# One product per block for both gates of the RG-LRU, smaller side steps and a later modulation deadline in a two-layer hybrid backbone

## The chip, the cores and the metric

The kernel runs on one core of a Trainium2 chip. The metric is the device time of one launch in microseconds: 1726.16 us is the median of three runs (1722.91 to 1727.71). TensorE (PE) multiplies matrices, with its weight loads shown apart (PEld); VectorE (DVE), ScalarE (ACT) and GpSimd (POOL) work on tiles in SBUF, DVE and ACT also on the banks of PSUM that PE writes; SyncE (SP) issues most of the loads.

## What is computed

Two layers with shared structure run over 384 tokens: 128 context tokens and 256 latent tokens. Each layer projects the normalized, modulated tokens (1024 wide) to 10240 columns, runs four branches (A neighbourhood attention, B differential attention, C retention, D RG-LRU), weighs each branch's projection by a sigmoid gate, sums them, multiplies by `w_out`, adds the residual, and then runs a squared-ReLU MLP. The part that the change rewrites is branch D:

```
def rglru_gates(x, wa, ba, wx, bx, lam):
    xb = xf.reshape(b, t, LRU_BLOCKS, -1)          # 8 blocks of 64 channels
    r = sigmoid(einsum('btnd,nde->btne', xb, wa).reshape(b, t, w) + ba)
    i = sigmoid(einsum('btnd,nde->btne', xb, wx).reshape(b, t, w) + bx)
    log_a = -LRU_C * r * softplus(-lam)
    a = exp(log_a)
    u = sqrt(-expm1(2.0 * log_a)) * (i * xf)
    return a, u
# h[t] = a[t] * h[t-1] + u[t], once forward and once backward; hd = h_f + h_b
```

`xf` is the input after a centred convolution of four taps. The modulation (shift, scale and gain from `silu(cond) @ ada_w + ada_b`) is a matrix-vector product for each of the two token groups.

## The kernel before, in words

**Products.** All big products (projections, gates, branches, `w_out`, MLP) are done in three passes on split operands: a float32 weight `raw` is cut into a high part `wh` and a rest `wl`, the tokens are held as `hh` and `hl` (or `yh`, `yl` for branch outputs), and PE adds hh·wh, hl·wh and hh·wl. ACT or DVE makes `wh`, DVE makes `wl`. Weights come in loads of 1 MB into two `raw` buffers, on SP's queue; a load is issued when the buffer before last has been split.

**Banks.** PSUM has six banks with the tag `y` and two with the tag `mm`. The projections and the branch products go to `mm`: PE can work on one bank while DVE or ACT reads the other, and it starts a third group only when the first has been read. In the gate and branch products ACT makes `th` (the tanh of a gate) out of its bank, and DVE makes `acc` or `th` times the branch product out of another.

**The stream and the side steps.** A list of pieces in a fixed order (`run_stream`) issues the big products. Everything else, attention, retention, RG-LRU and modulation, is written as Python generators (`later`, `active`); `poll` advances them between the pieces, up to their next `yield`. It decides by a model of the engines' clocks (`Clock`, `Engine.cost`): it takes no step while DVE or ACT stand more than `BACKLOG` = 2.25 us ahead of PE in that model. What a generator issues between two yields is one step, and stands in each engine's queue without anything between. Each engine runs its queue in order, so the order is fixed when the program is built. `drain_side(tag)` finishes all steps with a tag: a deadline.

**RG-LRU.** `lx_evac` copies a projection out of its bank and convolves it on DVE (one multiply, three multiply-adds) into `setB_x`. For each of four pairs of blocks j and two directions d, `lru_tile` makes two gates m; each gate has one bank, and two products of 64x64 weights, which lie at the two diagonal corners of the array (`tile_position=(r, r)`). ACT applies tanh with the bias `hb` to 128 partitions, then come exp, tanh, square and square root on ACT and the two recurrences on DVE (`tensor_tensor_scan`). Multiply, scans, sums and the product with the gelu gate are one step. The gate weights lie in the tiles `bia`.

**Modulation.** `ada` streams `ada_w` in pieces of 256 KB into `half` tiles and accumulates on DVE (`big<-half,condT,big`); `ada_end` sums over the partitions on PE (`ones`), adds the bias, transposes. `need_y` of the layer's last branch drains it and issues the loads of the residual tokens (`load_x_tile`, three of 512 KB) and of the gains (`gain_tiles`, four of 256 KB); both are used after the product with `w_out`, whose last four slices are done by `out_tail`.

Of the kernel before, what the change touches and what calls it, by code (L numbers as in the profile page):

```python
# [140 lines left out]
class Engine:  # L141


    def __init__(self, clock, raw, key):
        self.clock, self.raw, self.key = clock, raw, key

    def __getattr__(self, name):
        f = getattr(self.raw, name)
# [18 lines left out]
    def cost(self, name, aps, k):  # L167
        if name == "dma_start":
            return 0.06
        n = max(_size(x) for x in aps)  # L170
        psum = any(x.space == PSUM for x in aps)
        if self.key == "ACT":
            return (0.05 if psum else 0.094) + n / 1200 + 0.09 * (len(aps) - 2)
        if self.key == "POOL":
            if k.get("op") == ALU.pow:
                return 0.3 + 0.16 * n
            return 0.1 + n / (290 if name == "tensor_copy" else 470)
        if self.key == "PE":
            n = _size(aps[0])
            if name == "transpose":  # L180
                return 0.107
            if aps[1].dtype == F32R:
                return max(n / 2195, 0.107)
            return max(n / 585, 0.22) * (aps[0].shape[0] / 128 if "tile_position" in k else 1)
        if name == "reciprocal":
            return 0.07 + n / 120
        extra = 0.06 * sum(x.shape[-1] == 1 for x in aps[1:])
        if name in ("tensor_scalar", "tensor_copy") and not psum:
            return 0.07 + n / 1920 + extra
        return 0.07 + n / 960 + extra  # L190
# [8 lines left out]
def hybrid_flow_kernel(ctx: ExitStack, tc: tile.TileContext, I, O):  # L199
# [162 lines left out]
    def stage_params():  # L362
# [72 lines left out]
        for l in range(DEPTH):  # L435
            pp = pps[l]
            li = 0.8 - 0.6 * math.exp(-0.3 * l)
            nlam = cp.tile([128, 1], F32, name=f"nlam{l}")
            dve.tensor_sub(nlam, e2[:, 2 * l + 1:2 * l + 2], e2[:, 2 * l:2 * l + 1])
            dve.tensor_scalar(nlam, nlam, -li, None, op0=ALU.add)  # L440
            hb = cp.tile([128, 24], F32, name=f"hb{l}")
            dve.tensor_scalar(hb, pp[:, R_BAF:R_BAF + 24], 0.5, None, op0=ALU.mult)
            dn = cp.tile([128, 1], F32, name=f"dn{l}")
            dve.tensor_scalar(dn, pp[:, R_DN:R_DN + 1], 1.0 - li, None, op0=ALU.mult)
            rn = cp.tile([128, 4], F32, name=f"rn{l}")
            dve.tensor_scalar(rn, pp[:, R_RN:R_RN + 4], 0.5, None, op0=ALU.mult)
# [10 lines left out]
            LP[l].update(nlam=nlam, hb=hb, dn=dn, rn=rn, lg=lg, nlb=nlb, lgc=lgc, zt=zt,  # L457
                         kl=lp[:, 32 + 8 * l:40 + 8 * l].rearrange("p (d j) -> p d j", d=2))
            yield

# [473 lines left out]
    def add_layer(l):  # L934
# [206 lines left out]
        def lx_evac(j, p):  # L1141
            xp = atile()
            pool.memset(xp[:, 0:1], 0.0)
            pool.memset(xp[:, 129:131], 0.0)
            pool.memset(xp[:, 387:389], 0.0)
            dve.tensor_copy(xp[:, 1:129], p[:, 0:128])
            dve.tensor_copy(xp[:, 131:387], p[:, 128:384])
            xd = ctile("setB_x")
            cw = lambda i: P("pp")[:, R_CW + 4 * i + j:R_CW + 4 * i + j + 1]
            dve.tensor_scalar(xd[:, 0:NL], xp[:, 0:NL], cw(0), P("pp")[:, R_CB + j:R_CB + j + 1], op0=ALU.mult, op1=ALU.add)  # L1150
            for i in range(1, 4):
                dve.scalar_tensor_tensor(xd[:, 0:NL], xp[:, i:NL + i], cw(i), xd[:, 0:NL], op0=ALU.mult, op1=ALU.add)
            S["xd"][j] = xd

        def gelu(a, gv):
# [17 lines left out]
            if j == 3:  # L1173
                later(S["split_yD"](), "yD")

        def lru_w(m):

            return S["bia"][m][:, 128:384].rearrange("p (j e) -> p j e", j=4)

        def lru_load():  # L1180
            S["bia"] = [stile([128, 640], "bia", 4) for _ in range(4)]
            for b in S["bia"]:
                pool.memset(b[:, 0:128], 0.0)
                pool.memset(b[:, 512:640], 0.0)
            for m, n in enumerate(("lru_wa_fwd", "lru_wx_fwd", "lru_wa_bwd", "lru_wx_bwd")):
                SP.dma_start(lru_w(m), I[n][l].rearrange("(j q) d e -> (q d) j e", q=2))

        def lru_tile(j):
            xd = S["xd"][j][:, 0:NL]
            while "kl" not in LP[l]:  # L1190
                yield
            yield (xd, *S["bia"])
            hst = S["hst"]
            A, U, Sq = [], [], []
            for d in range(2):
                base = 12 * d
                ths = []
                for m in range(2):
                    p = bank()[:, 0:NL]
                    w = lru_w(2 * d + m)  # L1200
                    for r in (slice(0, 64), slice(64, 128)):
                        mm(p[r], w[r, j], xd[r], start=True, stop=True, tile_position=(r.start, r.start))
                    th = tmp()[:, 0:NL]
                    act(th, p, AF.Tanh, scale=0.5, bias=P("hb")[:, base + 4 * m + j:base + 4 * m + j + 1])
                    ths.append(th)
                kl = P("kl")[:, d, j:j + 1]
                L, u = ths
                yield (L, u)
                dve.tensor_scalar(L, L, kl, kl, op0=ALU.mult, op1=ALU.add)
# [16 lines left out]
            for d in range(2):  # L1226
                u = U[d]
                dve.tensor_mul(u, u, Sq[d])
                h = Sq[d]
                st = P("pp")[:, (R_SF, R_SB)[d] + j:(R_SF, R_SB)[d] + j + 1]  # L1230
                for s, init in ((slice(0, 128), 0.0), (slice(130, 386), st)):
                    aa, uu, oo = A[d][:, s], u[:, s], h[:, s]
                    if d:
                        aa, uu, oo = aa[:, ::-1], uu[:, ::-1], oo[:, ::-1]
                    dve.tensor_tensor_scan(oo, aa, uu, init, ALU.mult, ALU.add)
                hs.append(h)
            pool.tensor_copy(hst[:, j:j + 1], hs[0][:, 127:128])
            pool.tensor_copy(hst[:, 4 + j:5 + j], hs[1][:, 0:1])
            gg = S["gg"][j]
            for s, o in ((slice(0, 128), slice(0, 128)), (slice(130, 386), slice(128, 384))):  # L1240
                dve.tensor_add(hs[0][:, s], hs[0][:, s], hs[1][:, s])
                dve.scalar_tensor_tensor(gg[:, o], hs[0][:, s], 0.5, gg[:, o], op0=ALU.mult, op1=ALU.mult)
            S["yD"][j] = gg[:, 0:NTOK]
            if j == 3:
                later(hst_out(hst), "out")
# [44 lines left out]
        def ret_pair(j):  # L1290
# [3 lines left out]
            for hh in range(2):  # L1294
# [4 lines left out]
                dve.scalar_tensor_tensor(a, rel, P("lg")[:, 0, h:h + 1], a, op0=ALU.mult, op1=ALU.min)  # L1299
                act(a, a, AF.Exp)  # L1300
                Dm.append(a)
            qx = []
            io = cst[:, C_IO:C_IO + 256]
            for d in range(2):
# [201 lines left out]
        def add_gate_branch(bi, ykey, first, last):  # L1506
# [15 lines left out]

            def need_y():
                drain_side(ykey)
                if last:
                    drain_side("ada")
                    S["X"] = [load_x_tile(l, t) for t in range(3)]
                    S["G"] = gain_tiles(l, 1)
                    S["A2"], S["B2"] = scale_cols(MOD[l, 4], pps[l], R_FFN), MOD[l, 3]

            def piece(dd):
                def fn(hi, lo):
# [31 lines left out]
        def out_mm(k, t, hi, lo, banks=(0, 1)):  # L1564
            mh, ml = S["M"]
            tk = slice(t * 128, (t + 1) * 128)
            for n in banks:
# [2 lines left out]
                mm(p, ml[:, k, tk], wh, start=False, stop=False)  # L1570
                mm(p, mh[:, k, tk], wl, start=False, stop=k == KT - 1)

        def add_out():
            def piece(k):
                def fn(hi, lo):
# [7 lines left out]
            for k in range(0, KT, 2):  # L1583
                src = I["w_out"][l][k * 128:(k + 2) * 128].rearrange("(k p) c -> p k c", p=128)
                add_load(src, lambda raw: raw.rearrange("p (k c) -> p k c", k=2),
                         [((lambda v, s=s: v[:, s]), (lambda t: t), piece(k + s), None)
                          for s in range(2)])
            tail = loads[-2]["pieces"][0]
            tail["home"], loads[-2]["pieces"][1]["home"] = home_bia, home_sbd
# [193 lines left out]
    MOD = {}  # L1783
# [134 lines left out]
```

## Time and profile before

| | |
|---|---|
| median of three runs | 1726.16 us |
| the profiled execution | 1721.72 us |
| its span, first to last instruction | 1719.9 us (mean granted PE clock 0.99) |
| PE busy | 1661.3 us, 97% |
| PE weight loads | 1492.2 us, 87% |
| DVE busy | 1170.9 us, 68% |
| ACT busy | 697.2 us, 41% |
| POOL busy | 227.7 us, 13% |
| moved by DMA | 250.84 MB, 146 GB/s |

Matmuls are pipelined, so a busy PE is one with a matmul in flight; what counts is where it stands still or runs at the lower of its two clocks. A timeline row gives the start, the busy time, the engine, the operation with its output and inputs, how many were merged (x), and in brackets the idle time before it and what ended that. A matmul of plain float32 shows as two records. Line numbers are those of a helper that issues everything (L151), so one reads by tile names.

### The profile page before, as it was taken

The page shows a single profiled execution, that of the slowest core. Times are in us where ns is not written, and L with a number is a line of the kernel's source. Part 1 is how long each engine was busy: PE and PEld are TensorE (multiplying, and loading weights), DVE is VectorE, ACT ScalarE, POOL GpSimd, SP SyncE. Part 2 cuts the span into 40 slices and gives each one's busy share as a digit, 9 for nine tenths or more (in the row PEclk, how much of TensorE's full clock was granted, in tenths as well). Part 3 has the DMA queues.
Part 4 walks back from the last instruction along what each step waited for, and adds up shares of the span by engine and source line. Part 5 has one row for each costly group of instructions (what it writes and reads, how often), then busy time and mean ns, then how long its engine had stood idle before and what let it go on. Part 6 is the DMA issues. An engine that isn't in the chain of part 4 may idle for free.

```text
span 1719.9 us, 24255 instructions
## 1 busy us (share of the span) xinstructions
PE 1661.3 (97%) x9370; PEld 1492.2 (87%) x9370; DVE 1170.9 (68%) x2030; ACT 697.2 (41%) x1352; POOL 227.7 (13%) x298
## 2 busy tenths in 40 slices
PE   6999989999999999999999999999999999999998
PEld 4989879889789899898899887898888998898997
DVE  4586578998565746877677866787786666475444
ACT  4335555233332543333362446532343337333333
POOL 3211000322220100000021200013412101000000
PEclk8999999999999999999999999999999999999999
DMA  9432234458425425665453322453673442454332
GB/s 348 137 105 80 98 100 164 163 169 206 100 99 184 147 93 171 213 208 183 162 165 105 104 99 74 147 179 133 174 210 84 138 169 99 134 202 154 123 123 86
DMA packets 181124, 250.84 MB, mean 146 GB/s; under 512 B 21777, under 2 KB 126018, under 8 KB 181010
## 3 DMA queue, kind: packets, MB, share of 16 engines
q1 hardware_dynamic: 167234, 240.66, 41.1%
q0 software_dynamic: 3936, 5.94, 2.8%
q10 hardware_dynamic: 9840, 2.71, 0.7%
q8 instruction: 73, 1.20, 0.3%
q14 instruction: 41, 0.34, 0.1%
HBM read 243.47 MB, written 5.81 MB: 145 GB/s over the span
## 4 chain that ended last, share of the span: by engine, by line
PE 81%; DVE 8%; DMA 4%; ACT 3%; issue 3%; POOL 1%; SPq 0%; DVEq 0%; ACTq 0%; POOLq 0%
PE mm L151 48%; PE y L151 33%; DVE wl L151 2%; DMA half<-in_ada_w 2%; DVE tmp L151 2%; DVE big L151 1%; ACT tmp L151 1%; DMA half<-in_ada_b 1%; DMA wh<-in_ada_w 1%; ACT wh L151 1%; DVE half L151 1%; DVE setB_x L151 0%; ACT half L151 0%; DVE acc L151 0%; DVE small L151 0%
## 5 line engine op out<-in xcount | busy, mean ns | idle before, releaser
L151 PE MATMUL mm<-hh,wh 128*128 128x384 f32 x1536 | 537.2, 350 | 23.0 <-DVE acc L151 18.0
L151 PE MATMUL mm<-hh,wl 128*128 128x384 f32 x1536 | 520.7, 339 | 1.3 <-DVE wl L151 1.3
L151 PE MATMUL mm<-hl,wh 128*128 128x384 f32 x1536 | 520.4, 339 | 0.0
L151 DVE TENSOR_TENSOR wl<-raw,wh 128x1024 fp32r<-128x1024 f32 x313 | 394.4, 1262 | 163.2 <-ACT wh L151 155.5
L151 ACT ACTIVATE wh<-raw 128x1024 fp32r<-128x1024 f32 x249 | 262.2, 1055 | 224.9 <-PE y L151 139.7
L151 PEld LDWEIGHTS mm<-hh,wh 128*128 128x128 f32 x1536 | 290.7, 189 | 50.2 <-issue 21.1
L151 PEld LDWEIGHTS mm<-hl,wh 128*128 128x128 f32 x1536 | 290.6, 189 | 1.6
L151 PEld LDWEIGHTS mm<-hh,wl 128*128 128x128 f32 x1536 | 290.1, 189 | 1.6 <-DVE wl L151 1.6
L151 DVE SCALAR_TENSOR_TENSOR big<-half,condT,big 128x512 f32<-128x512 f32 x224 | 160.8, 755 | 15.0 <-DMA half<-in_ada_w 14.9
L151 PE MATMUL y<-wh,yh 128*128 128x512 f32 x312 | 123.4, 396 | 0.0
L151 PE MATMUL y<-wh,yl 128*128 128x512 f32 x312 | 123.4, 396 | 0.0
L151 PE MATMUL y<-wl,yh 128*128 128x512 f32 x312 | 123.3, 395 | 0.0
L151 PE MATMUL mm<-yh,wh 128*128 128x384 f32 x256 | 89.5, 350 | 3.2 <-DVE th L151 3.0
L151 POOL TENSOR_TENSOR small<-small,mhalf 128x1 f32<-128x1 f32 (+2 forms) x40 | 35.2, 883 | 413.2 <-DVE small L151 413.2
L151 DVE CAST wh<-raw 128x1024 fp32r<-128x1024 f32 x67 | 46.4, 692 | 61.0 <-PE mm L151 57.3
L151 PE MATMUL mm<-yh,wl 128*128 128x384 f32 x256 | 86.3, 337 | 0.0
L151 PE MATMUL mm<-yl,wh 128*128 128x384 f32 x256 | 86.2, 337 | 0.0
L151 ACT ACTIVATE tmp<-mm 128x384 f32<-128x384 f32 x64 | 31.4, 491 | 135.1 <-PE mm L151 135.1
L151 PE MATMUL y<-wh,hh 128*128 128x512 f32 (+1 forms) x192 | 76.0, 396 | 0.2 <-DVE hh L151 0.2
L151 PE MATMUL y<-wh,hl 128*128 128x512 f32 (+1 forms) x192 | 73.7, 384 | 0.3 <-DVE hl L151 0.3
L151 PE MATMUL y<-wl,hh 128*128 128x512 f32 (+1 forms) x192 | 73.6, 383 | 0.0
L151 PEld LDWEIGHTS y<-wl,yh 128*128 128x128 f32 x312 | 58.6, 188 | 14.1
(327 smaller groups left out, 2496.8 us busy)
## 6 DMA issues: line engine op xcount, KB each, us to landing
raw<-in_w_in SPq DMA_DIRECT2D x80, 1024.0 KB
raw<-in_mlp_w SPq DMA_DIRECT2D x64, 1024.0 KB
half<-in_ada_w SPq DMA_DIRECT2D x160, 256.0 KB
raw<-in_w_branch SPq DMA_DIRECT2D x16, 1024.0 KB
raw<-in_w_out SPq DMA_DIRECT2D x8, 1024.0 KB
v<-gscr SPq DMA_DIRECT2D x16, 256.0 KB
bia<-in_na_rpb POOLq DMA_DIRECT2D x32, 96.0 KB, 7.2
raw<-in_ada_w SPq DMA_DIRECT2D x4, 512.0 KB
```

What stands on the lines that cost most here:

```text
L151: r = f(*a, **k)
```

## The change

Each of the 16 pairs of blocks and directions of a kernel now takes two products of 64 rows and 128 columns: both gates' weights of a block stand side by side, and the two blocks of a pair lie in the upper and the lower half of the array's rows and write two banks. A bank then holds both gates of one block, so ACT reads each half of each bank apart and writes the halves of the two gate tiles; where a half moves to the other 64 partitions, the bias comes from a copy with swapped halves, `hbs`. The convolution leaves `lx_evac` and is a side step in two parts; the recurrences, the sums and the preparation of retention's decay have more yields. The loads of tokens and gains move from the last branch's first piece to the first piece of the product with `w_out`. The planner's costs of PE are other ones.

```diff
@@ Engine.cost, PE
-                return max(n / 2195, 0.107)
-            return max(n / 585, 0.22) * (aps[0].shape[0] / 128 if "tile_position" in k else 1)
+            place = (aps[1].start_partition(), aps[0].start_partition())
+            switch = 0.0 if cut == self.cut else 0.1
+            t = 0.107 if name == "transpose" else max(n / 2195, 0.107) if aps[1].dtype == F32R else max(n / 612, 0.22)
...
+            return switch + (0.014 if beside else t)
@@ stage_params
+            hbs = cp.tile([128, 2, 8], F32, name=f"hbs{l}")
+            for r in range(0, 128, 64):
+                SP.dma_start(hbs[r:r + 64], hb[64 - r:128 - r].rearrange("p (d c) -> p d c", d=2)[:, :, 0:8])
@@ lx_evac
+            later(conv(j, xp), "yD")
+
+        def conv(j, xp):
+            yield (xp,)
             xd = ctile("setB_x")
...
                 dve.scalar_tensor_tensor(xd[:, 0:NL], xp[:, i:NL + i], cw(i), xd[:, 0:NL], op0=ALU.mult, op1=ALU.add)
+                if i == 1:
+                    yield
@@ lru_load
-                SP.dma_start(lru_w(m), I[n][l].rearrange("(j q) d e -> (q d) j e", q=2))
+                for jh in range(2):
+                    dst = S["bia"][m // 2 * 2 + jh][:, 128:384].rearrange("p (j g e) -> p j g e", j=2, g=2)[:, :, m % 2]
+                    SP.dma_start(dst, I[n][l, 4 * jh:4 * jh + 4].rearrange("(j q) d e -> (q d) j e", q=2))
@@ lru_tile
-                for m in range(2):
-                    p = bank()[:, 0:NL]
-                    w = lru_w(2 * d + m)
-                    for r in (slice(0, 64), slice(64, 128)):
-                        mm(p[r], w[r, j], xd[r], start=True, stop=True, tile_position=(r.start, r.start))
-                    th = tmp()[:, 0:NL]
-                    act(th, p, AF.Tanh, scale=0.5, bias=P("hb")[:, base + 4 * m + j:base + 4 * m + j + 1])
-                    ths.append(th)
+                rs = (slice(0, 64), slice(64, 128))
+                pb = [bank()[:, 0:NL] for _ in rs]
+                for r, p in zip(rs, pb):
+                    mm(p, lru_w(d, j)[r], xd[r], start=True, stop=True)
+                ths = [tmp()[:, 0:NL] for _ in range(2)]
+                for q in range(2):
+                    for m in range(2):
+                        b = P("hb")[rs[m], base + 4 * m + j:] if q == m else P("hbs")[rs[m], d, 4 * m + j:]
+                        act(ths[m][rs[q]], pb[q][rs[m]], AF.Tanh, scale=0.5, bias=b[:, 0:1])
...
                 hs.append(h)
+                yield
...
                 dve.scalar_tensor_tensor(gg[:, o], hs[0][:, s], 0.5, gg[:, o], op0=ALU.mult, op1=ALU.mult)
+                yield
@@ ret_pair
                 Dm.append(a)
+                yield
@@ need_y -> need_x, called before the first piece of add_out
-                if last:
-                    drain_side("ada")
-                    S["X"] = [load_x_tile(l, t) for t in range(3)]
-                    S["G"] = gain_tiles(l, 1)
-                    S["A2"], S["B2"] = scale_cols(MOD[l, 4], pps[l], R_FFN), MOD[l, 3]
```

How this moves instructions is seen at two places. On DVE, the end of the first RG-LRU tile of the first layer stood between two readings of `mm` banks (`acc<-th,mm`) as one run of a weight split (`wl`), two multiplies, four scans (printed as SCALAR_TENSOR_TENSOR on `tmp`), two sums and two products (`setB_g`):

```order
L151 SCALAR_TENSOR_TENSOR acc<-th,mm 128x384
L151 TENSOR_TENSOR wl<-raw,wh 128x1024
L151 TENSOR_TENSOR tmp<-tmp 128x386
L151 SCALAR_TENSOR_TENSOR tmp<-tmp 128x128
L151 SCALAR_TENSOR_TENSOR tmp<-tmp,pp_117 128x256
L151 TENSOR_TENSOR tmp<-tmp 128x386
L151 SCALAR_TENSOR_TENSOR tmp<-tmp 128x128
L151 SCALAR_TENSOR_TENSOR tmp<-tmp,pp_117 128x256
L151 TENSOR_TENSOR tmp<-tmp 128x128
L151 SCALAR_TENSOR_TENSOR setB_g<-tmp,setB_g 128x128
L151 TENSOR_TENSOR tmp<-tmp 128x256
L151 SCALAR_TENSOR_TENSOR setB_g<-tmp,setB_g 128x256
```

In the changed program the same work, on DVE at the same tile, is:

```order
L152 SCALAR_TENSOR_TENSOR acc<-th,mm 128x384
L152 TENSOR_TENSOR tmp<-tmp 128x386
L152 SCALAR_TENSOR_TENSOR tmp<-tmp 128x128
L152 SCALAR_TENSOR_TENSOR tmp<-tmp,pp_117 128x256
L152 TENSOR_TENSOR tmp<-tmp 128x386
L152 SCALAR_TENSOR_TENSOR tmp<-tmp 128x128
L152 SCALAR_TENSOR_TENSOR tmp<-tmp,pp_117 128x256
L152 SCALAR_TENSOR_TENSOR acc<-th,mm 128x384
L152 TENSOR_TENSOR wl<-raw,wh 128x1024
L152 TENSOR_TENSOR tmp<-tmp 128x128
L152 SCALAR_TENSOR_TENSOR setB_g<-tmp,setB_g 128x128
L152 TENSOR_TENSOR tmp<-tmp 128x256
```

A reading of a bank now stands behind the scans, and the weight split, the sums and the products come after it. Before, the whole run stood between two readings in three further tiles, one of this layer and two of the second; in the changed program it does so in none.

On SP, at the end of the first layer's last branch, the loads of tokens and gains stood ahead of the last branch weights:

```order
L151 DMA raw<-in_w_in 128x8x256 x2
L151 DMA big<-in_x_prompt 128x1024
L151 DMA big<-in_x_sample 128x1024 x2
L151 DMA v<-gscr_113 128x512 x4
L151 DMA raw<-in_w_branch 128x4x512
L151 DMA raw<-in_w_out 128x2x1024 x4
```

In the changed program, at the same place on SP:

```order
L152 DMA raw<-in_w_in 128x8x256 x2
L152 DMA raw<-in_w_branch 128x4x512
L152 DMA raw<-in_w_out 128x2x1024 x3
L152 DMA big<-in_x_prompt 128x1024
L152 DMA big<-in_x_sample 128x1024 x2
L152 DMA v<-gscr_113 128x512 x4
L152 DMA raw<-in_w_out 128x2x1024
```

Seven loads have moved past one load of branch weights and three of `w_out`, and now stand ahead of the fourth `w_out` load.

## Rows read from the trace of the kernel before

**Rows 1.** The page, part 1: busy time, share, instructions of each engine.
```profile
PE 1661.3 (97%) x9370; PEld 1492.2 (87%) x9370; DVE 1170.9 (68%) x2030; ACT 697.2 (41%) x1352; POOL 227.7 (13%) x298
```
**Rows 2.** Who PE waited for: us in total, times, longest.
```profile
PE mm L151 <- DVE acc L151: 18.0, 7, 3.9
PE y L151 <- DVE half L151: 6.9, 7, 3.1
PE mm L151 <- DVE th L151: 6.6, 6, 2.1
```
**Rows 3.** Timeline of PE around the first gate products: start, us, idle before.
```profile
202.30 0.34 PE L151 MATMUL mm<-hh,wl 128*128 128x384 f32 x1
202.57 1.51 PE L151 MATMUL y<-setB_x,bia 64*64 64x386 f32 x8
204.02 0.44 PE L151 MATMUL mm<-hh,wh 128*128 128x384 f32 x1
204.29 0.34 PE L151 MATMUL mm<-hl,wh 128*128 128x384 f32 x1
```
**Rows 4.** Timeline of PE around two heads of neighbourhood attention.
```profile
415.53 0.34 PE L151 MATMUL mm<-hh,wl 128*128 128x384 f32 x1
415.79 0.71 PE L151 MATMUL y<-setB_g,setB_x 64*128 64x256 f32 x4
416.33 0.39 PE L151 MATMUL y<-kctx,setB_x 64*128 64x128 f32 x4
416.65 0.44 PE L151 MATMUL mm<-hh,wh 128*128 128x384 f32 x1
416.94 0.33 PE L151 MATMUL mm<-hl,wh 128*128 128x384 f32 x1
```
**Rows 5.** Timeline of PE: a float32 product on all rows.
```profile
57.59 0.59 PE L151 MATMUL y<-setA_q,cst 128*128 128x256 f32 x2
...
58.20 0.33 PE L151 MATMUL mm<-hl,wh 128*128 128x384 f32 x1
```
**Rows 6.** Timeline of PE: matmuls that waited.
```profile
106.58 0.41 PE L151 MATMUL mm<-hh,wh 128*128 128x384 f32 x1 [1.49 <-DVE acc L151]
...
220.66 0.69 PE L151 MATMUL mm<-hh,wh 128*128 128x384 f32 x1 [3.28 <-DVE acc L151]
...
446.93 0.66 PE L151 MATMUL y<-ident,half 128*128 128x128 f32 x4 [3.12 <-DVE half L151]
...
1180.83 0.41 PE L151 MATMUL mm<-hh,wh 128*128 128x384 f32 x1 [2.06 <-DVE th L151]
```
**Rows 7.** Timeline of DVE ahead of the matmul at 220.66.
```profile
214.48 1.23 DVE L151 TENSOR_TENSOR wl<-raw,wh 128x1024 fp32r<-128x1024 f32 x1 [0.68 <-ACT wh L151]
215.62 0.56 DVE L151 TENSOR_TENSOR tmp<-tmp 128x386 f32<-128x386 f32 x1
...
218.75 0.27 DVE L151 TENSOR_TENSOR tmp<-tmp 128x128 f32<-128x128 f32 x1
...
220.06 1.01 DVE L151 SCALAR_TENSOR_TENSOR acc<-th,mm 128x384 f32<-128x384 f32 x2
```
**Rows 8.** Stretches: us, busy of PE, PEld, DVE, ACT, POOL, granted clock, DMA, GB/s.
```profile
219.43:226.26 6.83, 5.60 (x16) 3.16 (x17) 3.22 (x6) 1.24 (x4) 0.00 (x0) 0.50 0.11 42
...
1065.94:1069.35 3.41, 3.41 (x12) 2.02 (x13) 1.26 (x2) 0.10 (x1) 0.00 (x0) 0.50 0.00 0
```
**Rows 9.** ACT by line and shape: busy us, mean ns, idle before.
```profile
L151 ACT ACTIVATE tmp<-y,hb 128x386 f32<-128x386 f32 x32 | 18.7, 584 | 27.9 <-PE y L151 27.0
```
**Rows 10.** Loads of `w_out`: SP's timeline, then ACT's.
```profile
562.21 6.63 SPq L151 DMA_DIRECT2D raw<-in_w_out  x2
...
573.50 2.05 ACT L151 ACTIVATE wh<-raw 128x1024 fp32r<-128x1024 f32 x2 [4.13 <-DMA raw<-in_w_out]
```
**Rows 11.** The chain that ended last: start, us, the product with `w_out`.
```profile
562.08 21.71 PE y L151 x93
```
**Rows 12.** A stretch as in rows 8: the loads of tokens and gains.
```profile
526.10:535.10 9.00, 9.00 (x54) 9.00 (x53) 5.53 (x11) 1.55 (x2) 0.00 (x0) 1.00 0.89 311
```

More of the change, by code (lines that the diff above doesn't have):

```diff
@@ L145, in __init__ @@
         self.clock, self.raw, self.key = clock, raw, key
+        self.cut, self.places = (128, 128), []
     def __getattr__(self, name):
@@ L179, in cost @@
             n = _size(aps[0])
+            cut = tuple(next(x for x in (32, 64, 128) if a.shape[0] <= x) for a in (aps[1], aps[0]))
             if name == "transpose":
-                return 0.107
-            if aps[1].dtype == F32R:
-                return max(n / 2195, 0.107)
-            return max(n / 585, 0.22) * (aps[0].shape[0] / 128 if "tile_position" in k else 1)
+                cut = (128, 128)
+            place = (aps[1].start_partition(), aps[0].start_partition())
+            switch = 0.0 if cut == self.cut else 0.1
+            t = 0.107 if name == "transpose" else max(n / 2195, 0.107) if aps[1].dtype == F32R else max(n / 612, 0.22)
+            if switch or cut == (128, 128) or place in self.places:
+                self.places = []
+            beside = bool(self.places)
+            self.cut = cut
+            self.places.append(place)
+            return switch + (0.014 if beside else t)
         if name == "reciprocal":
@@ L456, in stage_params @@
             act(zt, zt, AF.Exp)
-            LP[l].update(nlam=nlam, hb=hb, dn=dn, rn=rn, lg=lg, nlb=nlb, lgc=lgc, zt=zt,
+            LP[l].update(nlam=nlam, hb=hb, hbs=hbs, dn=dn, rn=rn, lg=lg, nlb=nlb, lgc=lgc, zt=zt,
                          kl=lp[:, 32 + 8 * l:40 + 8 * l].rearrange("p (d j) -> p d j", d=2))
@@ L1174, in lg_evac, with lru_w @@
                 later(S["split_yD"](), "yD")
-        def lru_w(m):
-            return S["bia"][m][:, 128:384].rearrange("p (j e) -> p j e", j=4)
+        def lru_w(d, j):
+            return S["bia"][2 * d + j // 2][:, 128 + j % 2 * 128:256 + j % 2 * 128]
         def lru_load():
@@ L1185, in lru_load @@
             for m, n in enumerate(("lru_wa_fwd", "lru_wx_fwd", "lru_wa_bwd", "lru_wx_bwd")):
-                SP.dma_start(lru_w(m), I[n][l].rearrange("(j q) d e -> (q d) j e", q=2))
+                for jh in range(2):
+                    dst = S["bia"][m // 2 * 2 + jh][:, 128:384].rearrange("p (j g e) -> p j g e", j=2, g=2)[:, :, m % 2]
+                    SP.dma_start(dst, I[n][l, 4 * jh:4 * jh + 4].rearrange("(j q) d e -> (q d) j e", q=2))
         def lru_tile(j):
+            while "kl" not in LP[l] or S["xd"][j] is None:
+                yield
             xd = S["xd"][j][:, 0:NL]
-            while "kl" not in LP[l]:
-                yield
             yield (xd, *S["bia"])
@@ L1196, in lru_tile @@
                 base = 12 * d
-                ths = []
-                for m in range(2):
-                    p = bank()[:, 0:NL]
-                    w = lru_w(2 * d + m)
-                    for r in (slice(0, 64), slice(64, 128)):
-                        mm(p[r], w[r, j], xd[r], start=True, stop=True, tile_position=(r.start, r.start))
-                    th = tmp()[:, 0:NL]
-                    act(th, p, AF.Tanh, scale=0.5, bias=P("hb")[:, base + 4 * m + j:base + 4 * m + j + 1])
-                    ths.append(th)
+                rs = (slice(0, 64), slice(64, 128))
[7 more added lines that the diff above has]
+                        act(ths[m][rs[q]], pb[q][rs[m]], AF.Tanh, scale=0.5, bias=b[:, 0:1])
                 kl = P("kl")[:, d, j:j + 1]
@@ L1301, in ret_pair @@
                 Dm.append(a)
+                yield
             qx = []
@@ L1571, in out_mm, with need_x @@
                 mm(p, mh[:, k, tk], wl, start=False, stop=k == KT - 1)
+        def need_x():
+            drain_side("ada")
+            S["X"] = [load_x_tile(l, t) for t in range(3)]
+            S["G"] = gain_tiles(l, 1)
+            S["A2"], S["B2"] = scale_cols(MOD[l, 4], pps[l], R_FFN), MOD[l, 3]
         def add_out():
@@ L1585, in add_out @@
                 add_load(src, lambda raw: raw.rearrange("p (k c) -> p k c", k=2),
-                         [((lambda v, s=s: v[:, s]), (lambda t: t), piece(k + s), None)
+                         [((lambda v, s=s: v[:, s]), (lambda t: t), piece(k + s), None if k + s else need_x)
                           for s in range(2)])
```

## The prediction

> **What bounds the kernel now.** I read the page first, then PE's waits, then the timeline around the longest of them, last the granted clock. PE is busy in 97% of the span [rows 1], and no other engine passes 68% (weight loads lie beside the matmuls). So only three things shorten this kernel: fewer PE cycles, fewer places where PE stands still, and less time at its lower clock. The page's 1661.3 us of busy time leave 58.6 us of standing still, in a span of 1719.9 us.
>
> The waits [rows 2] tell where: PE waited 18.0 us for `acc` and 6.6 us for `th`, both written by DVE when it reads an `mm` bank, and 6.9 us for DVE's `half`, the modulation's rows. The timeline [rows 6] shows that four of the waits for `acc` stand at the end of an RG-LRU tile (the first 3.28 us; with the longest, 3.9 in [rows 2], and two more like the first 13.7 us). The other three, 4.3 us, stand at the convolutions; the one at 106.58 is 1.49. The clock tells the rest: behind the wait that ended at 220.66 it was granted at 0.50, the 1.2 GHz level, for 6.83 us, and behind two further RG-LRU waits, the wait at 446.93 and the one at 1180.83 for 3.41 us each, as in the second line of [rows 8]. After 220.66 PE worked 5.6 us at half speed, which gives away 2.8; the other four stretches give away 1.7 each, so 9.6 us in all.
>
> **The change part by part.**
>
> *The gate products.* Between the starts at 202.30 and 204.29 stand one group of gate products and two ordinary products of 0.174 us (their spacing here: a 384-column product at full clock), so the group costs 1.99 - 0.35 = 1.64 us [rows 3]. There are 16 groups. The new group has two products of 64 rows and 128 columns in the two halves of the rows. The nearest rows are those of neighbourhood attention [rows 4]: two heads, each in its half of the rows, with 256 + 128 moving columns a head, cost 1.41 - 0.35 = 1.06 us including the changes to and from this shape. A float32 product of 256 columns on all rows costs 0.61 - 0.17 = 0.44 us [rows 5]; two such and two of half the length, one after another, would be 1.3 us alone, more than the whole group took, so the halves do run beside each other. A new group streams 386 columns a half instead of 384: 1.06 us, and 16 x 0.58 = 9.3 us go. From below: if the halves ran one after another, the streaming would be that of today: two products of 386 columns at 0.44/256 us a column, 1.33 us. With the change of shape of [rows 4] (1.06 less 384 columns, 0.66, so 0.40) that is 1.73, a loss of 16 x 0.09 = 1.4 us. From above, with today's change of shape (1.64 - 1.33 = 0.31) the group costs 0.97 and 10.7 go. I take 9.3.
>
> *ACT behind it.* A bank is now read in two halves of 64 partitions: 64 readings of 386 columns instead of 32, which took 584 ns each [rows 9]. Time goes by columns here, so I add 32 x 0.58 = 18.7 us to an engine that is 41% busy [rows 1]. A group's four readings (2.3 us) lie beside the gate projection, 24 products x 0.174 = 4.2 us, while ACT must also read that projection's bank. It fits mostly; I charge 1 us, with 0 and 18.7 as ends. The Trainium skill, "TensorEngine Tiling (Array Packing)", section "Performance Considerations", speaks against the change: tiling speeds up the products, not the emptying of PSUM, which may then bind. The trace shows ACT with that slack, so I take this as a rival only, at the price of all 32 added readings.
>
> *The end of the RG-LRU tile.* Before 220.66, DVE did a weight split and ten instructions from 214.48 to 220.06 between two bank readings: 5.6 us [rows 7]. PE stood from 217.38 on (220.66 - 3.28), so at this place it bears some 217.38 - 214.48 - 0.3 = 2.6 us of such work, the 0.3 for the end of the reading itself. In the new order the longest run is two multiplies and four scans, 215.62 to 218.75, 3.1 us; the sums with a weight split behind it are 1.3 + 1.1 = 2.4 us. That leaves perhaps 0.5 us in the first tile and, with the other places, 1.5 in all: 12.2 of 13.7 us go. The total work of DVE is the same, so from below I allow that half returns elsewhere: 6.
>
> *The convolution.* It leaves `lx_evac`, so that the bank reading of the next projection no longer stands behind four DVE instructions: the wait of 1.49 goes [rows 6]. The first of the three stands behind the preparation of parameters, which stays; of the remaining 2.8 us I count a third: 2.4 us in all, ends 0 and 4.3.
>
> *Modulation and the shorter decay step.* The deadline itself bound nothing before: tokens and gains were loaded at 526 us [rows 12], and the last transposes of the modulation stood at 446.93. That wait of 3.12 us [rows 6] is one of order: two bias additions of attention and the modulation's row on one DVE queue. The new order gives the last part of the modulation more products between its sum and its transposes, but the part before it stands as the last one did. I take 2 of 3.1 us, ends 0 and 4. Of the 6.6 us for `th`, the largest (2.06 at 1180.83, behind retention's decay) is cut by the new yield. Against that, in the new order a weight split and four modulation accumulations stand before a reading at two places, which is longer than anything but the RG-LRU run; I charge 2 us net, from -6 to +3.
>
> *The clock.* The three low stretches behind RG-LRU waits go with them: 2.8 + 1.7 + 1.7 = 6.2 us. Of the two others I count half, 1.7: 7.9 us, ends 3 and 9.6. The wait of 1.49 at 106.58 had no low stretch behind it.
>
> *The late loads.* Tokens and gains (2.62 MB) now stand ahead of the fourth load of `w_out`. Before, that one was issued at 568.5 and landed at 573.50 [rows 10]. PE did 96 products in the 21.71 us from 562.08 [rows 11] (72 of four slices, 24 of the first token tile; three records are missing), 0.226 us each, so the fourth load's first slice is due after 84, at 581.1. The stretch at 526 with these very loads moved 311 GB/s [rows 12]. From 562.2, 1.6 us of start-up (5.0 us for 1.05 MB, less 3.4) and 4.72 MB at that rate end at 579.0; with 2.2 us for the split (1.0 on ACT, 1.2 on DVE) 581.2. The cover is used up: I charge 0.5 us a layer, 1 in all, ends 0 and 8.
>
> The eight gate-weight loads in place of four, and the four for `hbs`, add about 2 us each to SP's queue where it waits for buffers anyway: nothing, and a few us at most if a `raw` load were late.
>
> Sum: 9.3 - 1 + 12.2 + 2.4 + 2 - 2 + 7.9 - 1 = 29.8 us. Against the profiled execution (1721.72 us, of which 1.8 lie around the span) that gives 1691.9. That execution was 4.4 us below the median of the runs, so against the median 1696.4.
>
> **The rivals.**
>
> *The waits come back in smaller pieces.* DVE does the same work between the same readings, and 2.25 us of backlog are still allowed before a step. If 16 of the 20.3 us (13.7 + 6.6) and 6 of the 9.6 us of clock stay, the change saves 9.3 + 4.3 + 3.6 + 2.4 - 2 = 17.6: 1708.6. For it: the waits of 2 us at steps as short as decay's. Against: the new runs between two readings are little over half of the old.
>
> *The halves take turns.* 9.3 + 1.4 = 10.7 us more than forecast: 1707.1. Only attention's rows [rows 4] speak on this, and against it.
>
> *ACT binds.* All added readings show: 17.7 us more, 1714.1. For it: the readings, exp, tanh and square of one direction are some 3.9 us on ACT, beside 4.2 + 1.06 us of PE. Against: ACT's idle time before these readings alone is 27.9 us [rows 9].
>
> *The late loads starve the product with `w_out`: slower.* At 124 GB/s, two fifths of the rate in [rows 12], the 4.72 MB end at 601.9, the slice is ready at 604.1, 23.0 us late; with a low clock behind it 24.7 us a layer, twice: 1696.4 - 1 + 49.4 = 1744.8. It outweighs the rest only below about 155 GB/s, half the rate that the same loads had.
>
> **How the numbers follow.** The forecast has 0.64, the smaller pieces 0.16, turns 0.06, ACT 0.08, starvation 0.06. 0.3%, about 5 us, is what a measurement of this kernel can tell from no change. Faster, below 1721, are the forecast and the first three rivals but for a few hundredths: 0.88. Same 0.06, slower 0.06. The forecast alone, with its ends partly combined, spans 1685 to 1706; taking in the first three rivals, the range is 1682 to 1714. The time is that of the forecast, 1696.
>
> **What would show it.** Right: the group's cost near 1.06 us at 16 places; PE's total wait for `acc` under 6 us; no low clock behind an RG-LRU tile; `w_out`'s fourth load landing near 579 with PE waiting less than 1 us. Wrong: a row of PE waiting for ACT's `tmp` or `th` at the tiles, new waits of 3 us for `th` beside the modulation with the clock at 0.50 behind them, or a wait for `wl` or `wh` near 580.

## The result, and the profile after

The changed kernel takes 1685.55 us (median of four runs, 1684.98 to 1687.72), the kernel before 1724.54 on the same chip: a ratio of 0.9776, 95% interval 0.9754 to 0.9798. That is 39.0 us less; the profiled spans fell by 36.7, from 1719.9 to 1683.2. The forecast was 1696, so the time lies in its range, near the lower end: the change did more than was counted.

PE's line on the page of the changed kernel answers to [rows 1]:

```profile
PE 1644.1 (98%) x9306; PEld 1484.2 (88%) x9306; DVE 1160.7 (69%) x2030; ACT 726.7 (43%) x1393; POOL 216.9 (13%) x289
```

Its gate group on the timeline of PE (start, us, operation; [rows 3] before):

```profile
193.01 0.34 PE L152 MATMUL mm<-hh,wl 128*128 128x384 f32 x1
193.28 0.92 PE L152 MATMUL y<-setB_x,bia 64*128 64x386 f32 x4
194.12 0.44 PE L152 MATMUL mm<-hh,wh 128*128 128x384 f32 x1
194.40 0.34 PE L152 MATMUL mm<-hl,wh 128*128 128x384 f32 x1
```

From 193.01 to 194.40 are 1.39 us; less two ordinary products (0.35) the group costs 1.05, where it was 1.64. All 16 groups measure within 0.01 of that at full clock: 9.5 us are gone.

Who PE waited for after (us in total, times, longest; [rows 2] before):

```profile
PE y L152 <- DVE half L152: 4.1, 5, 2.5
PE mm L152 <- DVE th L152: 3.7, 4, 1.8
PE mm L152 <- DVE wl L152: 2.5, 2, 2.0
...
PE mm L152 <- ACT tmp L152: 1.1, 1, 1.1
...
PE mm L152 <- DVE acc L152: 0.4, 1, 0.4
```

The row for `acc` fell from 18.0 to 0.4. DVE's timeline at the first RG-LRU tile shows why ([rows 7] before):

```profile
206.14 0.55 DVE L152 SCALAR_TENSOR_TENSOR acc<-th,mm 128x384 f32<-128x384 f32 x1
206.86 0.56 DVE L152 TENSOR_TENSOR tmp<-tmp 128x386 f32<-128x386 f32 x1 [0.18 <-ACT tmp L152]
...
209.36 0.73 DVE L152 TENSOR_TENSOR_SCAN tmp<-tmp,pp 128x256 f32<-128x256 f32 x1
210.00 0.53 DVE L152 SCALAR_TENSOR_TENSOR acc<-th,mm 128x384 f32<-128x384 f32 x1
210.44 1.22 DVE L152 TENSOR_TENSOR wl<-raw,wh 128x1024 fp32r<-128x1024 f32 x1
```

The reading at 210.00 no longer stands behind the split, the sums and the products. PE's wait there is the 0.4 of the list, and it is the only one left at an RG-LRU tile.

From the two traces the 36.7 us can be followed. For the part of the span behind the first 46 us, the groups give 9.5. PE's waits, added up over all its matmuls, fell from 37.2 to 18.0: 19.2. At the lower clock PE did 19.2 us of work before (five stretches) and 3.4 after (one stretch); half of that is lost, 9.6 against 1.7, so 7.9. Together 36.6. At 46 us the changed kernel was also nine products, 1.1 us, ahead, so the parts come to 1.0 more than the whole; where that was lost is not located.

| PE's waits behind the first 46 us | before | after | forecast gain | gain |
|---|---|---|---|---|
| ends of RG-LRU tiles | 13.7 | 0.4 | 12.2 | 13.3 |
| convolution | 4.3 | 0 | 2.4 | 4.3 |
| all others | 19.2 | 17.6 | -2 | 1.6 |

The -2 is the sum of four terms: ACT -1, modulation 2, `th` -2, late loads -1.

The one stretch of lower clock that is left (PE's wait, then us, busy of PE, PEld, DVE, ACT, POOL, granted clock, DMA, GB/s) follows a wait of 2.46 us for the modulation's row:

```profile
1217.18 0.68 PE L152 MATMUL y<-ident,half 128*128 128x128 f32 x4 [2.46 <-DVE half L152]
...
1217.68:1221.09 3.41, 3.41 (x13) 3.41 (x12) 3.31 (x9) 0.00 (x0) 0.00 (x0) 0.50 0.84 295
```

ACT's readings of the gate banks, by shape (busy, mean ns, idle before), answer to [rows 9]:

```profile
L152 ACT ACTIVATE tmp<-y,hbs 64x386 f32<-64x386 f32 x32 | 18.5, 579 | 0.6
L152 ACT ACTIVATE tmp<-y,hb 64x386 f32<-64x386 f32 x32 | 18.5, 578 | 12.9 <-PE y L152 12.5
```

They take 37.0 us, twice as long, as forecast. In the whole trace PE waited for ACT's `tmp` once, and that `tmp` is no reading of a gate bank: the last gate group stands 60 us earlier, at 1075.16.

```profile
1137.40 0.41 PE L152 MATMUL mm<-hh,wh 128*128 128x384 f32 x1 [1.06 <-ACT tmp L152]
```

PE's other waits for ACT, at 114 (0.7), 284 (1.0) and 306 (0.9), lie away from the gate groups too, as do the small ones behind `w_out`: the gate readings on ACT do not bind.

### The profile page after: what moved, and what is told of

It is laid out like the page before. It is cut to its first block, busy times and chain, and to the rows that moved or that the text cites. A ratio compares the mean times of both kernels' runs of the same rounds, so it can differ in the third digit from the quotient of the medians.

```text
span 1683.2 us, 24132 instructions
## 1 busy us (share of the span) xinstructions
PE 1644.1 (98%) x9306; PEld 1484.2 (88%) x9306; DVE 1160.7 (69%) x2030; ACT 726.7 (43%) x1393; POOL 216.9 (13%) x289
## 4 chain that ended last, share of the span: by engine, by line
PE 83%; DVE 6%; ACT 4%; DMA 3%; issue 2%; SPq 1%; POOL 1%; ACTq 0%; POOLq 0%; DVEq 0%
PE mm L152 50%; PE y L152 33%; DVE big L152 2%; DVE tmp L152 1%; DVE wl L152 1%; ACT tmp L152 1%; SPq L152 1%; DMA half<-in_ada_w 1%; ACT half L152 1%; DMA wh<-in_ada_w 1%; ACT wh L152 1%; DMA raw<-in_w_in 1%; DVE half L152 0%; POOL small L152 0%; DVE small L152 0%
## 5 line engine op out<-in xcount | busy, mean ns | idle before, releaser
L152 ACT ACTIVATE wh<-raw 128x1024 fp32r<-128x1024 f32 x262 | 275.9, 1055 | 221.9 <-PE y L152 137.4
L152 DVE SCALAR_TENSOR_TENSOR big<-half,condT,big 128x512 f32<-128x512 f32 x224 | 165.3, 776 | 13.4 <-DMA half<-in_ada_w 13.4
L152 PEld LDWEIGHTS y<-wh,yh 128*128 128x128 f32 x312 | 58.7, 188 | 13.9 <-issue 0.8
```

What stands on the lines that cost most here:

```text
L152: r = f(*a, **k)
```

## The experiments

Times are medians; each ratio is taken against runs of the kernel before on the same chip, whose medians were 1721.4 to 1724.6 us. "Waits" is PE's idle time and "low clock" the length of the stretches at 0.50 (half of PE's work in them is lost), both in us behind the first 46 us and without the end of the span; `acc` is the list's row.

| kernel | us | ratio (95%) | waits | acc | low clock |
|---|---|---|---|---|---|
| before | 1724.54 | 1 | 37.2 | 18.0 | 20.5 |
| changed | 1685.55 | 0.9776 (0.9754 to 0.9798) | 18.0 | 0.4 | 3.4 |
| products alone | 1705.55 | 0.9898 (0.9878 to 0.9917) | 30.6 | 5.5 | 10.2 |
| small steps alone | 1703.72 | 0.9892 (0.9871 to 0.9913) | 24.2 | 3.9 | 13.7 |
| planner costs alone | 1710.18 | 0.9920 (0.9894 to 0.9946) | 30.5 | 13.1 | 17.1 |
| changed, large steps | 1701.67 | 0.9874 (0.9854 to 0.9895) | 25.5 | 6.6 | 10.2 |
| before, backlog 2.0 | 1713.14 | 0.9934 (0.9913 to 0.9955) | 32.8 | 18.2 | 20.5 |
| before, backlog 2.5 | 1733.57 | 1.0054 (1.0038 to 1.0070) | 42.2 | 19.9 | 41.0 |
| changed, backlog 2.0 | 1694.21 | 0.9820 (0.9797 to 0.9843) | 25.3 | 2.6 | 10.2 |
| changed, backlog 2.5 | 1690.17 | 0.9798 (0.9774 to 0.9823) | 20.8 | 1.0 | 6.8 |
| changed, early deadline | 1680.66 | 0.9763 (0.9740 to 0.9785) | 16.6 | 0.4 | 3.4 |
| changed, one half | 1692.17 | 0.9826 (0.9804 to 0.9848) | 16.0 | 0 | 3.4 |
| changed, bias row early | 1690.99 | 0.9819 (0.9797 to 0.9841) | 19.6 | 0.4 | 6.8 |
| changed, old planner costs | 1719.32 | 0.9973 (0.9959 to 0.9987) | 33.9 | 3.9 | 23.9 |

**The products alone.** Into the kernel before went `lru_load`, the products and readings of `lru_tile`, and `hbs`:

```diff
-                        mm(p[r], w[r, j], xd[r], start=True, stop=True, tile_position=(r.start, r.start))
...
+                    mm(p, lru_w(d, j)[r], xd[r], start=True, stop=True)
```

> The kernel before with only the new gate products (weights side by side, two products of 64 rows and 128 columns, four half readings, the swapped bias); steps, planner costs and deadline as before. Theory (parts are independent): a group falls from 1.99 to 1.40 us between its neighbours, so 16 x 0.59 = 9.5 us go; the waits at the RG-LRU tiles stay (PE's total of waits stays near 51 us), about 1715 us (1711 to 1718). Rival, ACT binds: the 32 added readings show as waits of PE for tanh tiles and most of the gain is gone, about 1722 to 1730. Rival, order luck: the planner counts other durations, so waits move to other places, and the sum of the waits changes by over 8 us in either direction.

The group measured 1.05 us here too, but 17 us went, not 9.5, and the four waits at the RG-LRU tiles were gone although the large step was still whole. DVE's timeline there:

```profile
217.53 0.55 DVE L151 SCALAR_TENSOR_TENSOR acc<-th,mm 128x384 f32<-128x384 f32 x1
217.99 0.55 DVE L151 TENSOR_TENSOR tmp<-tmp 128x386 f32<-128x386 f32 x1
...
222.09 0.42 DVE L151 SCALAR_TENSOR_TENSOR setB_g<-tmp,setB_g 128x256 f32<-128x256 f32 x1
222.43 0.54 DVE L151 SCALAR_TENSOR_TENSOR acc<-th,mm 128x384 f32<-128x384 f32 x1
222.90 1.22 DVE L151 TENSOR_TENSOR wl<-raw,wh 128x1024 fp32r<-128x1024 f32 x1
```

The same ten instructions stand between two readings, but the split now follows the second reading. From 217.99 to 222.43 are 4.4 us, and PE did not wait. The theory missed, and of the rivals order luck comes nearest: the places of the waits moved, though their sum changed by 6.6 us, less than the 8 it named. Which of the planner's estimates moved the split was not tried.

**The small steps alone.**

```diff
+            later(conv(j, xp), "yD")
...
                 hs.append(h)
+                yield
```

> The kernel before with only the smaller steps (convolution as a side step in two parts, yields behind each recurrence, each sum and each decay); products, planner costs and deadline as before. Theory (the steps remove the waits): waits for acc fall from 18.0 to under 3 us, four low clock stretches (6 to 8 us) go: 1724.5 - 16 - 7 = about 1701 us (1696 to 1707). Rival (the planner's costs remove the waits): under 8 us of gain, over 1716 us, waits for acc still over 10 us.

The theory held for the time (1703.7 in 1696 to 1707) and nearly for `acc` (18.0 to 3.9, under 3 was expected). The low clock fell by 7 us only, since new waits came elsewhere, the longest of 5.25 us for a modulation row.

**The planner's costs alone.**

```diff
-            return max(n / 585, 0.22) * (aps[0].shape[0] / 128 if "tile_position" in k else 1)
...
+            return switch + (0.014 if beside else t)
```

> The kernel before with only the planner's new costs of PE. Theory (the steps remove the waits): the order changes, but the long runs on DVE stay; waits for acc stay above 10 us and the time within 6 us of before, about 1724 us (1718 to 1730). Rival (the planner's costs remove the waits): over 15 us of gain, below 1710 us.

Neither held: 12.4 us went. Two of the four RG-LRU waits stayed (3.25 and 3.42), the two of the first layer went. The instructions are those of the kernel before, so this is one more order of them.

**The changed kernel with the large steps.** The hunks of `lx_evac`, of the end of `lru_tile` and of `ret_pair` are taken back:

```diff
                 hs.append(h)
-                yield
...
```

> The changed kernel with the old, large steps (convolution inside the reading of the bank, no added yields); new products, new planner costs and the late deadline stay. Theory (the steps remove the waits): the RG-LRU waits and their low clock come back, 13.7 + 4.3 + 7 = 25 us: about 1710 us (1703 to 1716), waits for acc over 12 us. Rival (the planner's costs remove the waits): within 6 us of the changed kernel, below 1692 us.

The time lies in between: taking the steps out of the changed kernel costs 16 us, not 25. The RG-LRU waits did not come back; those of the convolutions did (1.87, 2.09).

**One number of the planner**, in either kernel; the instructions are the same, their order is not:

```diff
-    BACKLOG = 2.25
+    BACKLOG = 2.0
```

> The kernel before with one number changed: the allowed backlog of the planner is 2.0 us instead of 2.25. It computes the same with the same instructions, only in another order. Theory (the four RG-LRU waits are an accident of one order; any edit that shuffles it removes some): the time falls by 5 to 18 us, to 1705 to 1718, waits for acc 4 to 14 us. Rival (the large steps cause the waits wherever they stand): within 5 us of before, waits for acc 15 us and more.

> The kernel before with the allowed backlog at 2.5 us. Theory (accident of one order): the time falls by 3 to 15 us, to 1708 to 1720, since a larger backlog lets more work pile up between two readings; waits for acc 6 to 16 us. Rival (the large steps cause the waits wherever they stand): within 5 us of before or slower, waits for acc 15 us and more.

> The changed kernel with the allowed backlog at 2.0 us: another order of the same instructions. Theory (the small steps make the order harmless): within 6 us of 1685.5, waits for acc under 3 us, no low clock at the RG-LRU tiles. Rival (the changed order was a lucky one): 8 us slower and more, above 1693, with waits of 2 to 3 us for acc or th at new places.

> The changed kernel with the allowed backlog at 2.5 us. Theory (the small steps make the order harmless): within 6 us of 1685.5, waits for acc under 3 us. Rival (the changed order was a lucky one): 8 us slower and more, above 1693.

In the kernel before the time went to 1713 or 1734 by this number, but the waits at the four tiles stayed; PE's timeline with 2.5:

```profile
220.10 0.69 PE L151 MATMUL mm<-yh,wh 128*128 128x384 f32 x1 [3.27 <-DVE acc L151]
...
257.88 0.69 PE L151 MATMUL mm<-yh,wh 128*128 128x384 f32 x1 [3.28 <-DVE acc L151]
...
1075.46 0.41 PE L151 MATMUL mm<-hh,wh 128*128 128x384 f32 x1 [3.77 <-DVE acc L151]
...
1112.74 0.41 PE L151 MATMUL mm<-hh,wh 128*128 128x384 f32 x1 [3.77 <-DVE acc L151]
```

So those waits were no accident of one order, as the theory had it; the rest of the change in time came with the order. In the changed kernel no such wait came with either number (the worst at a tile is 0.81), but with 2.0 the time missed the theory's 6 us and fell where the rival had it (1694.2), by waits of 1.8 to 2.8 us for modulation rows, weight splits and once `th`; with 2.5 the theory held (1690.2, `acc` 1.0).

Over all traces of this document PE's wait goes with the work that DVE has between two readings around an RG-LRU end, but is not fixed by it. 6.0 us of DVE's time (split, two multiplies, four scans, two sums, two products) always gave 3.25 to 3.92; 4.8 (without the split) gave nothing at three places and 2.13 at a fourth; 3.4 (two multiplies, four scans) gave 0 to 0.8, and twice 1.31 in the kernel with the old planner costs below; under 2.4 gave at most 0.2. The two that stand out, on PE's timelines of the kernel before with 2.0 and of the changed one with old costs:

```profile
1060.34 0.59 PE L151 MATMUL mm<-yh,wh 128*128 128x384 f32 x1 [2.13 <-DVE acc L151]
...
214.74 0.44 PE L151 MATMUL mm<-yh,wh 128*128 128x384 f32 x1 [1.31 <-DVE acc L151]
```

**The early deadline.** `need_x` goes back into the last branch's first piece; the rest is the changed kernel, with nearly its order:

```diff
             def need_y():
                 drain_side(ykey)
+                if last:
+                    drain_side("ada")
+                    S["X"] = [load_x_tile(l, t) for t in range(3)]
...
```

> The changed kernel with only the deadline of the modulation and the loads of tokens and gains back at the last branch; 110 of PE's rows differ in order. Theory A (the late loads cost something): in the trace after, each layer loses 2.0 us between the product with w_out and the first product of the MLP; with early loads these come back: 1681 to 1683.5 us, and the transposes of the normalised rows stand earlier. Theory B, mine in the prediction (the loads are hidden, at most 0.5 us a layer): 1684 to 1686.5. Theory C (the early deadline brings back a wait of 3 us for the modulation's row beside the last branch): 1687 to 1691.

Theory A by size, just below its range (1680.7): each layer got back 1.9 us between the product with `w_out` and the MLP. But the data had not been late. In the changed kernel SP's loads and ACT's split of the fourth `w_out` load stand so (SP's timeline, then ACT's):

```profile
539.31 0.37 SPq L152 DMA_DIRECT2D raw<-in_w_out  x1
...
545.73 0.38 SPq L152 DMA_DIRECT2D raw<-in_w_out  x1
...
553.80 2.01 ACT L152 ACTIVATE wh<-raw 128x1024 fp32r<-128x1024 f32 x2 [7.27 <-DMA raw<-in_w_out]
```

It landed 14.5 us after the first of these issues (forecast 16.8), and PE never waited for it. The normalisation of the first token tile begins at 561.66 after and at 563.80 with the early deadline, where everything is 2.15 us later: at the same place. What differs is the order behind it. In the changed kernel the last transposes come when few products are left beside them (PE's timeline):

```profile
580.02 1.09 PE L152 MATMUL y<-ident,half 128*128 128x128 f32 x8 [0.48 <-DVE half L152]
581.46 1.09 PE L152 MATMUL y<-ident,half 128*128 128x128 f32 x8 [0.34 <-DVE half L152]
582.88 0.65 PE L152 MATMUL y<-ident,half 128*128 128x128 f32 x4 [0.33 <-ACT half L152]
583.88 0.39 PE L152 MATMUL mm<-wh,hh 128*128 128x256 f32 x1 [0.35 <-ACT hh L152]
584.69 0.38 PE L152 MATMUL mm<-wh,hl 128*128 128x256 f32 x1 [0.42 <-DVE hl L152]
```

These waits are 1.9 us; with the early deadline the stretch has two, as before the change:

```profile
571.51 0.66 PE L152 MATMUL y<-ident,half 128*128 128x128 f32 x4 [0.77 <-DVE half L152]
...
584.89 0.66 PE L152 MATMUL y<-ident,half 128*128 128x128 f32 x4 [0.17 <-DVE half L152]
```

So 1.0 of the 1.9 us won are waits; the rest stands in no wait of the view and was not traced. The planner moved the row work; which of its estimates did it was not tried. Theory C had a part of the truth: the early deadline lost 2.1 us near 451 and won about 2.0 near 1217, both mostly by a stretch at 0.50 that came or went. In all its span is 3.8 us shorter. It is the fastest kernel here, though its interval overlaps that of the changed one; so the late deadline, a part of the change, gained nothing that these runs show.

**Both products in one half.** The second block's product takes the first one's rows, so the second block's gates are replaced by the first's. The planner's place of a product is changed along with it, so that it still counts the two as lying beside each other and draws the same order:

```diff
-            place = (aps[1].start_partition(), aps[0].start_partition())
+            place = (aps[1].start_partition(), aps[0].start_partition() + (id(aps[0]) if n == 386 else 0))
...
-                    mm(p, lru_w(d, j)[r], xd[r], start=True, stop=True)
+                    mm(p, lru_w(d, j)[rs[0]], xd[rs[0]], start=True, stop=True)
```

> The changed kernel with both gate products of a pair taken from the upper 64 rows (the second block then computes the first one's values); the same instructions in the same order, only the second product has lost its own half of the rows. Theory (the halves run beside each other): the group rises from 1.40 us to about 1.73, since 772 columns then pass one after another at 0.44/256 us a column: 16 x 0.33 = 5.3 us more, 1691 (1688 to 1694). Rival (the halves take turns already): the group stays at 1.40 us and the time within 1.5 us of 1685.5.

```profile
193.41 0.34 PE L152 MATMUL mm<-hh,wl 128*128 128x384 f32 x1
193.67 1.56 PE L152 MATMUL y<-setB_x,bia 64*128 64x386 f32 x4
195.16 0.44 PE L152 MATMUL mm<-hh,wh 128*128 128x384 f32 x1
195.44 0.34 PE L152 MATMUL mm<-hl,wh 128*128 128x384 f32 x1
```

From 193.41 to 195.44 are 2.03 us, 0.64 more than with two halves: one whole product of 386 columns (0.66 at [rows 5]'s 0.44 for 256). The expected rise from 1.40 to 1.73 mixed a figure with the neighbours' 0.35 and one without; the rise is from 1.05 to 1.69, beside the 1.73 of the prediction. The median rose by 6.6 us and the span by 7.2, not by the 10.2 of 16 such groups, since the span had 3.2 us less of waits. So with a half of the rows for each product the two run beside each other.

**The bias row early.** The wait at 1217.18 ended with the load of a bias; it is issued one weight slice earlier:

```diff
+                    if (k, u) == (KT - 2, 1):
+                        br = half()
...
+                            POOL.dma_start(br[32 * q::64], I["ada_b"][l, n * 1024:n * 1024 + 1024].rearrange("(u c) -> u c", u=2))
```

> The changed kernel with the modulation's bias row loaded one slice of weights earlier, so that the addition behind the sum over partitions no longer waits for that load. Theory (PE's wait of 2.46 us at 1217.18 is the load's 2.45 us, and the low clock behind it another 1.7): both go, 4 us, 1681.5 us (1679 to 1684). Rival (order luck: the step shuffles the order): the wait goes there, but others come, 1684 to 1692.

The rival won. That wait is gone, and others came with the new order, the largest on PE's timeline with 6.8 us of low clock around it:

```profile
1211.14 0.69 PE L152 MATMUL mm<-hh,wl 128*128 128x384 f32 x1 [3.47 <-DVE wl L152]
```

**The old planner costs.** Everything else of the change is in:

```diff
-            return switch + (0.014 if beside else t)
...
+            return max(n / 585, 0.22) * (aps[0].shape[0] / 128 if "tile_position" in k else 1)
```

> The changed kernel with only the planner's old costs of PE; products, steps and late deadline as changed. Alone, the new costs made the kernel before 12 us faster. Theory (they are one more shuffle of the order, and what they removed there the steps remove too): 1680 to 1693 us, waits for acc under 4 us, no low clock at the RG-LRU tiles. Rival (the new costs carry a gain of their own, since the planner now knows PE's time): 8 us slower than the changed kernel and more, 1694 to 1700, with waits of 2 us and more beside the modulation and attention.

The rival's time came, and by far more than it said: 1719.3, only 0.3% below the kernel before. The group still costs 1.05 us and `acc` only 3.9, so products and steps do what they did; 16 us of waits, most of them not for `acc`, and 20 us of low clock have come back. That the new costs gain because they are truer, as the rival has it, one order cannot show. The largest wait is at the modulation of the first layer, on PE's timeline:

```profile
453.21 1.12 PE L151 MATMUL y<-ident,half 128*128 128x128 f32 x4 [5.24 <-DVE half L151]
```

The longest stretch of lower clock stands in retention, behind waits of 1.8 and 1.3 us:

```profile
288.30:298.54 10.24, 8.90 (x39) 8.82 (x39) 7.09 (x16) 0.70 (x3) 0.16 (x1) 0.50 0.62 229
```

## Why the prediction was right, and where it was short

The sum was 29.8 us and 39.0 went. In the profiled executions, with 36.7, the terms compare so:

- *The gate products* are right: 1.05 us against 1.06, 9.5 us against 9.3, and the halves work beside each other, as attention's heads [rows 4] had shown. The bound for halves in turn, 1.73, is close to the 1.69 measured for one half.
- *ACT* is right: the added readings cost 18.3 us of ACT (forecast 18.7), and no wait of PE stands at them (1 us was charged). The warning of the Trainium skill, "TensorEngine Tiling (Array Packing)", section "Performance Considerations", holds in its first half, since the readings of the banks gained nothing from the pairing; they did not become the bound.
- *The end of the RG-LRU tile* is right in place and size: 3.4 us of work between two readings left 0.4 us, forecast 0.5; 13.3 of 13.7 us went. Half right in cause: with the steps no tile end cost more than 1.5 us in any order tried, but the products alone removed these waits too, by putting the split elsewhere. One term may not be given to one edit.
- *The clock* is right in sum, 7.9 as forecast, and in its parts by luck. The three stretches behind RG-LRU waits went, as said; of the two others both went, not half, and a new one of 1.7 us came at 1217.68.
- *The convolution* went whole, 4.3 instead of 2.4: the preparation of parameters before the first one did not keep its wait.
- *Modulation and `th`* is the term that missed most in size: with ACT and the late loads it was to lose 2 us and won 1.6. The wait at 446.93 [rows 6] went. The new wait behind four modulation accumulations was foreseen, and here it is on DVE, then on PE:

```profile
446.38 3.79 DVE L152 SCALAR_TENSOR_TENSOR big<-half,condT,big 128x512 f32<-128x512 f32 x4 [1.34 <-DMA half<-in_ada_w]
450.10 0.54 DVE L152 SCALAR_TENSOR_TENSOR th<-th,mm 128x384 f32<-128x384 f32 x1
...
450.70 0.45 PE L152 MATMUL mm<-hh,wh 128*128 128x384 f32 x1 [1.81 <-DVE th L152]
```

It cost 1.8 us, with no low clock behind it, but `th` in all fell from 6.6 to 3.7 and `half` from 6.9 to 4.1, where a net loss was charged. (The prediction takes all 6.9 us for `half` as the modulation's rows; 1.9 of them stood at the transposes behind `w_out`.)

- *The late loads* lost 1.9 us a layer against the early deadline, not 0.5, and not by the mechanism charged: the loads were in time, the row work was ordered worse.
- *What the prediction did not price at all* is the planner's new costs. It could leave them out of the sum, since it read the places off the final order; but it then explained that order by the steps. Taken singly, the products, the steps and the costs give 17.0, 18.8 and 12.4 us, 48 together, where the whole gives 39: in part they remove the same waits. With the old costs products, steps and late deadline together give 4. In that kernel three of the prediction's signs of being right hold (the group at 1.05 us, `acc` under 6 us, no low clock behind an RG-LRU tile), and the time is 1719 us. So the sum is right as an account of this one order; that products and steps bring such a gain in any order is not shown.

What stays open: whether the new costs are better because they are truer or because the orders drawn with them were. For the new gate group the old costs count 1.32 us and the new ones 0.85, both switches included, where PE took 1.05: at this group neither is clearly truer. Five kernels with new products, small steps and new costs lie between 1681 and 1694 us; with the old costs there is one, at 1719. Four orders of the kernel before, one of them drawn with the new costs, lie between 1710 and 1734.

## What to carry to other kernels

Where an order is planned from estimated costs, any edit redraws it. Here a change of the planner alone moved the time by 5 to 12 us, and once by 34: shake a number of the planner in both kernels before a gain of that size is given to an edit. A long step does harm by what it adds up to with its neighbours between two readings of PSUM, so cut it until the worst neighbour beside it still fits under the work that the banks hold. Small products of half the rows can be worth pairing in the two halves: here the second one cost no time that shows, and the doubled readings were free on an engine with slack.

## What the runs showed of the hardware

The second gate product, in its own half, took no time that shows (1.05 us a group), in the same half 0.64 us. ACT's readings of 386 columns took 584 ns on 128 partitions and 579 on 64.

The lower clock also followed short waits. In the changed kernel with large steps a wait of 1.87 us was followed by a stretch at 0.50, the 1.2 GHz level, from 101.7 on for 3.4 us:

```profile
100.23 0.41 PE L152 MATMUL mm<-hh,wh 128*128 128x384 f32 x1 [1.87 <-DVE acc L152]
```

In the kernel before, a wait of 1.88 us that ended at 100.25 was followed by none, and in the changed kernel neither were those of 1.81 and 2.04 us.
